# Scan states from split operands, and a new order around them, in an SSM block followed by an attention and recurrence block

## The chip, the cores and the metric

The kernel runs on one core of a Trainium2 chip. The metric is the device time of one execution in microseconds (us); the kernel before takes 2063.22 us (median of three runs, 2062.61 to 2064.13). Work is spread over engines that each run their own instructions in the order in which they are written: TensorE (PE: matmuls; PEld: its weight loads), VectorE (DVE), ScalarE (ACT), GpSimd (POOL) and SyncE (SP), which here issues nearly all DMAs.

## The reference

Two blocks over 512 positions of width 2048, in float32. What the change touches is the first block's mixer: a projection, a causal convolution with silu, and a scan over chunks that is computed with matmuls. For each group (8 of them, 8 heads each, one B and one C per group):

```
cs = cumsum(ac)                                     # per chunk
decay = exp(where(mask, cs[:, None] - cs[None, :], -inf))
y_diag = (C B^T) * decay @ xdt
y_off  = C @ state * exp(cs)
state  = state * exp(cs[-1]) + B^T @ (xdt * exp(cs[-1] - cs))
y = y_diag + y_off + d_skip * x;   y = y * silu(z)
```

The second block needs mod = silu(c) @ w_ada + b_ada, a vector of 6144 numbers, for shift, scale and gate. It does not depend on x, so the kernel computes it beside the first block.

## The kernel before, in words

Large products are exact to nearly float32 by splitting: each operand is written as hi (float32r, a ScalarE copy, L171) plus lo (the rest, a VectorE subtraction, L172), and three float32r matmuls make one product: hi*hi, hi*lo, lo*hi (L197 to L199, in `gemm`). Weights come in blocks of 512 KB (tile `raw`), and each block gives two pairs hi, lo; three buffers of each are in use, so that ScalarE's next hi copy waits until TensorE is through with the pair of three copies ago. A gemm of two output tiles (`g`) runs over 16 steps of the contraction, kt = 0 to 15, six matmuls each.

The first part works through 8 groups. Each group has five gemms: B and C; then for the first half of its heads x and z; then for the second half x and z. I call each half a unit, numbered 0 to 15: unit 2g is group g's first half, 2g+1 its second. The scan of unit u is put between the gemms:

- `bc_late`: transposes B (`btp`), copies it to `btok` (L517), and makes C B^T (`cbp`), masked into `cbm`. It stands at kt = 11 of the first x gemm of a group.
- `ssd_pre`: transposes x (`tp`), and makes xdt (x times dt) and xdw (x times the weight of the position at its chunk's end). `ssd_decay` makes the masked decays `dec` and the `cex` on ScalarE and VectorE. `ssd_states` multiplies btok with xdw for three chunks (float32 matmuls into `sa` and `sb`, L1149) and carries the state from chunk to chunk on VectorE: a multiplication by `exl` (L1157) and an addition (L1159) per chunk, into `st`. They stand at kt = 11, 12 and 14 of the unit's z gemm (in unit 0 at kt = 5, 6 and 9 of a later gemm).
- `ssd_unit`, after the z gemm: 56 small matmuls into `yp`, chunk 3 first: first those of dec and xdt (L1198), then those of cex and st (L1200). The first L1200 needs the last state, so the end of the chain of three states.

`ada(n)` takes n rows of w_ada (tile `adaw`, two buffers) and makes each a column of mod with one VectorE instruction of 1024 columns (L1226) behind the last lo. At its first and 49th row it loads c, and makes silu of it on ScalarE and VectorE (L1217 to L1221). There are two or three rows per gemm.

The program is recorded in this order, and a scheduler orders each engine's instructions by its own estimate of when each can start; `issue_after` and `high_priority` bind or favour some. PSUM pools: `pg` (the gemms), `pa` (tp, sa, sb, btp, cbp and others) and `py` (yp), two buffers each.

Of the kernel before, what the change touches and what calls it, by code (L numbers as in the profile page):

```python
# [6 lines left out]
F32 = mybir.dt.float32  # L7
F32R = mybir.dt.float32r
I32 = mybir.dt.int32
AF = mybir.ActivationFunctionType  # L10
# [130 lines left out]
class _K:  # L141
    def __init__(self, tc, I, O, dbg):
        self.tc, self.nc, self.I, self.O, self.dbg = tc, tc.nc, I, O, dbg
        self.n = 0

# [32 lines left out]
    def gemm(self, chunks, acts, ncol=2, nk=4, tag=0, before=None, early=True, after=None):  # L178
        nc = self.nc
        ps = [self.pg.tile([P, S], F32, tag=f"g{j + tag}", name=self.nm("g")) for j in range(ncol)]  # L180
        self.mms = []
        nkt = len(chunks) * nk
        kt = 0
        width = ncol * P
        for src in chunks:
            if before:
                before(kt)
            hl = self.wchunk(src, width * nk, early=early)
            for k in range(nk):
                if after:  # L190
                    after(kt)
                a = acts[kt]
                hi, lo = hl[k * 2 // nk]
                for j in range(ncol):
                    o = k % (nk // 2) * width + j * P
                    c = slice(o, o + P)
                    nc.tensor.matmul(ps[j], hi[:, c], a[:, 0, :], start=kt == 0, stop=False)  # L197
                    nc.tensor.matmul(ps[j], hi[:, c], a[:, 1, :], start=False, stop=False)  # L198
                    mm = nc.tensor.matmul(ps[j], lo[:, c], a[:, 0, :], start=False, stop=kt == nkt - 1)  # L199
                    self.mms.append(mm.ins)  # L200
                kt += 1
        assert kt == nkt
        return ps
# [160 lines left out]
    def part1(self):  # L364
# [138 lines left out]
        for g in range(NG):  # L503
# [6 lines left out]
            btok = tmp.tile([P, 3, P], F32, tag="btok", name=f"btok{g}", bufs=1)  # L510
            cbm = tmp.tile([P, NC, P], F32, tag="cbm", name=f"cbm{g}", bufs=1)

            def bc_late(g=g, bt=bt, ct=ct, btok=btok, cbm=cbm):
                btp = self.pa.tile([P, NC, P], F32, tag="a", name=f"btp{g}")
                for c in range(3):
                    nc.tensor.transpose(btp[:, c, :], bt[:, c * P : c * P + P], self.ckc("ident"))
                nc.scalar.activation(btok, btp[:, 0:3, :], AF.Copy)  # L517
                cbp = self.pa.tile([P, NC, P], F32, tag="a", name=f"cbp{g}")
                for c in range(NC):
                    nc.tensor.matmul(cbp[:, c, :], bt[:, c * P : c * P + P], ct[:, c * P : c * P + P],  # L520
                                     start=True, stop=True)
                nc.vector.tensor_tensor(cbm, cbp, self.ckc("triu").unsqueeze(1).to_broadcast([P, NC, P]), ALU.mult)
# [9 lines left out]
            for u in range(2):  # L532
# [21 lines left out]
                if g or u:  # L554
                    mid.update({11: steps[0:1], 12: steps[1:2], 14: steps[2:3]})
                    late.append(unit)
                else:
                    slow = {1: [bc_late], 5: steps[0:1], 6: steps[1:2], 9: steps[2:3]}
# [558 lines left out]
    def ssd_pre(self, g, u, xs, pre):  # L1117
# [5 lines left out]
        xdw = tmp.tile([P, 3, 4, 64], F32, tag="xdw", name=self.nm("xdw"), bufs=1)  # L1123
        for c2 in range(2):
            tp = self.pa.tile([P, 2, 4, 64], F32, tag="a", name=self.nm("tp"))
            for c in range(2):
                for j in range(2):
# [7 lines left out]
            nc.vector.tensor_tensor(xdw[:, a:b2], tp[:, 0 : b2 - a],  # L1135
                                    self.dtw[:, a:b2, h0 : h0 + 4].unsqueeze(3).to_broadcast([P, b2 - a, 4, 64]),
                                    ALU.mult)
        pre.update(csr=csr, xdt=xdt, xdw=xdw)


    def ssd_states(self, g, u, btok, pre):
# [6 lines left out]
        for c in range(3):  # L1148
            nc.tensor.matmul(parts[c].rearrange("p h d -> p (h d)"), btok[:, c, :],  # L1149
                             xdw[:, c].rearrange("p h d -> p (h d)"), start=True, stop=True)  # L1150
        st = []
        for c in range(3):
            ns = self.tmp.tile([P, 4, 64], F32, tag="st", name=self.nm("st"), bufs=3)
            if c == 0:
                nc.scalar.activation(ns, parts[0], AF.Copy)
            else:
                nc.vector.tensor_tensor(  # L1157
                    ns, st[-1], self.exl[:, c, h0 : h0 + 4].unsqueeze(2).to_broadcast([P, 4, 64]), ALU.mult)
                nc.vector.tensor_tensor(ns, ns, parts[c], ALU.add)  # L1159
# [26 lines left out]
    def ssd_unit(self, g, u, xs, pre, yg):  # L1186
# [4 lines left out]
        for c in (3, 2, 1, 0):  # L1191
            cl = slice(c * P, c * P + P)
            for part in range(2 if c else 1):
                for h in range(4):
# [6 lines left out]
                    prev = mm.ins  # L1201
        for j in range(2):
            nc.vector.scalar_tensor_tensor(yg[j], xs[j], self.pk("dskip", (g * 4 + u * 2 + j)), yp[j],
                                           ALU.mult, ALU.add)

    def ada(self, n):

        nc, I = self.nc, self.I
        for _ in range(n):
# [4 lines left out]
            kh, f = divmod(i, 48)  # L1214
            if f == 0:
                cb = self.tmp.tile([P, 1024], F32, tag="adac", name=self.nm("adac"), bufs=1)
                nc.sync.dma_start(cb, I["cvec"][kh].to_broadcast([P, 1024]))  # L1217
                th = self.tmp.tile([P, 1024], F32, tag="adaw", name=self.nm("adat"))
                nc.scalar.activation(th, cb, AF.Tanh, scale=0.5)
                nc.vector.scalar_tensor_tensor(cb, th, 1.0, cb, ALU.add, ALU.mult)  # L1220
                nc.vector.tensor_scalar(cb, cb, 0.5, None, ALU.mult)  # L1221
                self.cb = cb
            raw = self.tmp.tile([P, 1024], F32, tag="adaw", name=self.nm("adaw"))
            nc.sync.dma_start(raw, I["wada"][kh, f])
            with self.tc.issue_after(self.last_lo):
                nc.vector.tensor_tensor_reduce(out=raw, in0=raw, in1=self.cb, op0=ALU.mult, op1=ALU.add,  # L1226
                                               scale=1.0, scalar=0.0, accum_out=self.macc[:, i : i + 1])
            if i == 95:
# [23 lines left out]
```

## Time and profile before

| | |
|---|---|
| median of three runs | 2063.22 us |
| profiled execution | 2065.37 us |
| its span, first to last instruction | 2063.6 us |
| PE busy | 2042.9 us (99%) |
| DVE busy | 1316.8 us (64%) |
| ACT busy | 930.7 us (45%) |
| mean granted TensorE clock | 0.998 |

The groups and their scans take the span from about 62 us to 1001 us. "Busy" counts an instruction from its start to its modelled end; matmuls overlap, so the time that one costs is read from start to start in the timeline. Line numbers are those of the kernel before.

### The profile page before, as it was taken

The page shows a single profiled execution, that of the slowest core. Times are in us where ns is not written, and L with a number is a line of the kernel's source. Part 1 is how long each engine was busy: PE and PEld are TensorE (multiplying, and loading weights), DVE is VectorE, ACT ScalarE, POOL GpSimd, SP SyncE. Part 2 cuts the span into 40 slices and gives each one's busy share as a digit, 9 for nine tenths or more (in the row PEclk, how much of TensorE's full clock was granted, in tenths as well). Part 3 has the DMA queues.
Part 4 walks back from the last instruction along what each step waited for, and adds up shares of the span by engine and source line. Part 5 has one row for each costly group of instructions (what it writes and reads, how often), then busy time and mean ns, then how long its engine had stood idle before and what let it go on. Part 6 is the DMA issues. An engine that isn't in the chain of part 4 may idle for free.

```text
span 2063.6 us, 26879 instructions
## 1 busy us (share of the span) xinstructions
PE 2042.9 (99%) x10000; PEld 1694.2 (82%) x10000; DVE 1316.8 (64%) x2312; ACT 930.7 (45%) x1747; POOL 45.2 (2%) x35
## 2 busy tenths in 40 slices
PE   8999999999999999999999999989999999999999
PEld 7888888888878888888788888878888888888887
DVE  6777777687777868777643545476666675754333
ACT  6473444444344443444432433344554554763222
POOL 0000000000000000000000000000000000000000
PEclk9999999999999999999999999999999999999999
DMA  7344555545454454444533332225222223233442
GB/s 231 111 158 156 178 173 186 170 153 180 157 184 157 171 177 160 163 164 133 175 126 119 114 100 94 81 97 159 90 70 72 72 80 96 87 112 109 145 143 92
DMA packets 93268, 278.31 MB, mean 135 GB/s; under 512 B 9873, under 2 KB 20113, under 8 KB 91089
## 3 DMA queue, kind: packets, MB, share of 16 engines
q1 hardware_dynamic: 92848, 276.59, 41.0%
q8 instruction: 78, 1.28, 0.2%
q14 instruction: 54, 0.43, 0.1%
q10 hardware_dynamic: 288, 0.01, 0.0%
HBM read 262.80 MB, written 12.71 MB: 134 GB/s over the span
## 4 chain that ended last, share of the span: by engine, by line
PE 94%; DVE 3%; ACT 2%; DMA 1%; issue 1%; ACTq 0%; DVEq 0%
PE g L197 27%; PE g L198 27%; PE g L199 27%; PE yp L1198 1%; PE yp L1200 1%; PE gt L266 1%; PE gt L268 1%; PE gt L267 1%; PE op L926 1%; PE g L217 1%; DVE lo L172 1%; PE g L218 1%; PE g L219 1%; PE tp L1129 1%; PE sa L1149 1%
## 5 line engine op out<-in xcount | busy, mean ns | idle before, releaser
L172 DVE TENSOR_TENSOR lo<-raw,hi 128x512 fp32r<-128x512 f32 (+2 forms) x704 | 476.3, 677 | 542.3 <-ACT hi L171 539.6
L171 ACT ACTIVATE hi<-raw 128x512 fp32r<-128x512 f32 (+2 forms) x704 | 426.9, 607 | 860.9 <-PE g L198 774.6
L197 PE MATMUL g<-hn,hi 128*128 128x512 f32 x1216 | 480.0, 395 | 0.0
L199 PE MATMUL g<-hn,lo 128*128 128x512 f32 x1216 | 474.2, 390 | 0.0
L198 PE MATMUL g<-hn,hi 128*128 128x512 f32 x1216 | 473.9, 390 | 0.0
L197 PEld LDWEIGHTS g<-hn,hi 128*128 128x128 f32 x1216 | 228.3, 188 | 48.9 <-issue 2.4
L199 PEld LDWEIGHTS g<-hn,lo 128*128 128x128 f32 x1216 | 228.2, 188 | 48.0 <-issue 0.2
L198 PEld LDWEIGHTS g<-hn,hi 128*128 128x128 f32 x1216 | 228.4, 188 | 46.5 <-issue 0.2
L198 PE MATMUL g<-h,hi 128*128 128x512 f32 x512 | 200.7, 392 | 0.8 <-DVE h L689 0.8
L199 PE MATMUL g<-h,lo 128*128 128x512 f32 x512 | 199.8, 390 | 0.0
L197 PE MATMUL g<-h,hi 128*128 128x512 f32 x512 | 199.6, 393 | 0.0
L199 PE MATMUL g<-ya,lo 128*128 128x512 f32 x512 | 199.5, 390 | 0.0
L197 PE MATMUL g<-ya,hi 128*128 128x512 f32 x512 | 199.5, 390 | 0.0
L198 PE MATMUL g<-ya,hi 128*128 128x512 f32 x512 | 199.5, 390 | 0.0
L1226 DVE CUSTOM_DVE_ANT_0 adaw<-adaw,adac 128x1024 f32<-128x1024 f32 x96 | 115.6, 1221 | 18.7 <-DMA adaw<-in_wada 18.7
L198 PEld LDWEIGHTS g<-h,hi 128*128 128x128 f32 x512 | 96.2, 188 | 22.6 <-DVE h L689 3.2
L199 PEld LDWEIGHTS g<-ya,lo 128*128 128x128 f32 x512 | 96.1, 188 | 20.4 <-DVE lo L172 0.3
L197 PEld LDWEIGHTS g<-h,hi 128*128 128x128 f32 x512 | 96.0, 188 | 20.2 <-ACT h L688 1.1
L197 PEld LDWEIGHTS g<-ya,hi 128*128 128x128 f32 x512 | 96.1, 188 | 20.1 <-issue 0.2
L199 PEld LDWEIGHTS g<-h,lo 128*128 128x128 f32 x512 | 96.1, 188 | 19.9
L198 PEld LDWEIGHTS g<-ya,hi 128*128 128x128 f32 x512 | 96.1, 188 | 19.8 <-issue 0.2
L337 DVE SCALAR_TENSOR_TENSOR xc<-pr,cwh,xc 128x511 f32<-128x511 f32 (+1 forms) x144 | 101.8, 745 | 0.0
(362 smaller groups left out, 2597.2 us busy)
## 6 DMA issues: line engine op xcount, KB each, us to landing
raw<-in_win SPq DMA_DIRECT2D x216, 512.0 KB, 3.5
adaw<-in_wada SPq DMA_DIRECT2D x96, 512.0 KB, 4.6
raw<-in_wout SPq DMA_DIRECT2D x88, 512.0 KB, 3.5
csr<-csd SPq DMA_DIRECT2D x16, 1024.0 KB, 4.7
xT<-in_xT SPq DMA_DIRECT2D x16, 256.0 KB, 4.4
raw<-in_win SPq DMA_DIRECT2D x16, 256.0 KB, 3.6
ydram<-y SPq DMA_DIRECT2D x16, 256.0 KB, 2.1
yst<-ydram SPq DMA_DIRECT2D x8, 512.0 KB, 4.2
```

Source lines behind the costliest of these rows:

```text
L171: self.last_hi = nc.scalar.activation(hi, raw[:, i * h : i * h + h], AF.Copy).ins
L172: self.last_lo = nc.vector.tensor_tensor(lo, raw[:, i * h : i * h + h], hi.bitcast(F32), ALU.subtract).ins
L197: nc.tensor.matmul(ps[j], hi[:, c], a[:, 0, :], start=kt == 0, stop=False)
L198: nc.tensor.matmul(ps[j], hi[:, c], a[:, 1, :], start=False, stop=False)
L199: mm = nc.tensor.matmul(ps[j], lo[:, c], a[:, 0, :], start=False, stop=kt == nkt - 1)
L217: nc.tensor.matmul(ps[j], hi[:, o], a[:, 0, :], start=first, stop=False)
L218: nc.tensor.matmul(ps[j], hi[:, o], a[:, 1, :], start=False, stop=False)
L219: mm = nc.tensor.matmul(ps[j], lo[:, o], a[:, 0, :], start=False, stop=last)
L266: nc.tensor.matmul(ps[t], a[:, 0, ts], hi, start=k == 0, stop=False)
L267: nc.tensor.matmul(ps[t], a[:, 0, ts], lo, start=False, stop=False)
L337: nc.vector.scalar_tensor_tensor(xc[:, s:], ps[:, : S - s], w(k), xc[:, s:], ALU.mult, ALU.add)
L1226: nc.vector.tensor_tensor_reduce(out=raw, in0=raw, in1=self.cb, op0=ALU.mult, op1=ALU.add, scale=1.0, scalar=0.0, accum_out=self.macc[:, i ...
```

## The change

1. btok and xdw are split into hi and lo (float32r), and a product of the states is three float32r matmuls instead of one float32 matmul. New: a VectorE subtraction for btok; a float32 tile `xw` (one buffer), a ScalarE copy to hi and a VectorE subtraction to lo for each of the two pieces of xdw.
2. btp and cbp take buffers of `py` instead of `pa`.
3. The load of c for the second half of mod is issued at the 48th row, and that call of `ada` stops there; the silu of c is put behind the last lo.
4. In `ssd_states` the state instructions are recorded at high priority, and the first multiplication reads PSUM directly.
5. For second halves the three steps stand one kt earlier: 10, 11 and 13.
6. A fence: the first kt of the gemm after `ssd_unit` is issued behind the unit's last matmul.

```diff
@@ gemm
+                with self.tc.issue_after(self.fence) if self.fence is not None and kt == 0 else nullcontext():
...
+                self.fence = None
@@ part1
-            btok = tmp.tile([P, 3, P], F32, tag="btok", name=f"btok{g}", bufs=1)
+            btok = tmp.tile([P, 2, 3, P], F32R, tag="btok", name=f"btok{g}", bufs=1)
...
-                btp = self.pa.tile([P, NC, P], F32, tag="a", name=f"btp{g}")
+                btp = self.py.tile([P, NC, P], F32, tag="y", name=f"btp{g}")
...
-                nc.scalar.activation(btok, btp[:, 0:3, :], AF.Copy)
-                cbp = self.pa.tile([P, NC, P], F32, tag="a", name=f"cbp{g}")
+                nc.scalar.activation(btok[:, 0], btp[:, 0:3, :], AF.Copy)
+                nc.vector.tensor_tensor(btok[:, 1], btp[:, 0:3, :], btok[:, 0].bitcast(F32), ALU.subtract)
+                cbp = self.py.tile([P, NC, P], F32, tag="y", name=f"cbp{g}")
...
-                    mid.update({11: steps[0:1], 12: steps[1:2], 14: steps[2:3]})
+                    mid.update({10: steps[0:1], 11: steps[1:2], 13: steps[2:3]} if u else
+                               {11: steps[0:1], 12: steps[1:2], 14: steps[2:3]})
@@ ssd_pre
-            nc.vector.tensor_tensor(xdw[:, a:b2], tp[:, 0 : b2 - a],
+            xw = tmp.tile([P, 2, 4, 64], F32, tag="xw", name=self.nm("xw"), bufs=1)[:, 0 : b2 - a]
+            nc.vector.tensor_tensor(xw, tp[:, 0 : b2 - a],
...
+            nc.scalar.activation(xdw[:, 0, a:b2], xw, AF.Copy)
+            nc.vector.tensor_tensor(xdw[:, 1, a:b2], xw, xdw[:, 0, a:b2].bitcast(F32), ALU.subtract)
@@ ssd_states
-            nc.tensor.matmul(parts[c].rearrange("p h d -> p (h d)"), btok[:, c, :],
-                             xdw[:, c].rearrange("p h d -> p (h d)"), start=True, stop=True)
+            o = parts[c].rearrange("p h d -> p (h d)")
+            for i, (a, b) in enumerate(((0, 0), (0, 1), (1, 0))):
+                nc.tensor.matmul(o, btok[:, a, c, :], xdw[:, b, c].rearrange("p h d -> p (h d)"),
+                                 start=i == 0, stop=i == 2)
...
+            with self.tc.high_priority():
...
+                    nc.vector.tensor_tensor(ns, st[-1] if c > 1 else parts[0],
@@ ssd_unit
+        self.fence = prev
@@ ada
+            if i == 47:
+                self.ada_c(1)
+                return
```

Where instructions now stand, at three places. The first is VectorE in unit 2, from the last rows of mod in the z gemm to the last state. `adaw` are rows of mod, `lo` the gemm's lo tiles, the two `st` the second and third state, `zr` the first step on the z gemm's result. Before:

```order
L1226 ISA adaw_2052,macc<-adaw_2052,adac_1596 128x1024
L1226 ISA macc 128x1
L172 TENSOR_TENSOR lo_2064<-raw_2057,hi_2063 128x512
L1157 TENSOR_TENSOR st_1976<-st_1974,exl 128x256
L1159 TENSOR_TENSOR st_1976<-st_1976,sa_1969 128x256
L1157 TENSOR_TENSOR st_1979<-st_1976,exl 128x256
L1159 TENSOR_TENSOR st_1979<-st_1979,sb_1970 128x256
L567 TENSOR_TENSOR zr_2027<-g_1788,rb_602 128x512
```

The same place now (lines of the changed kernel: L173 is the lo, L1141 and L1145 the piece of xdw and its lo, L1168 and L1170 the states):

```order
L1244 ISA adaw_2087,macc<-adaw_2087,adac_1621 128x1024
L1244 ISA macc 128x1
L1141 TENSOR_TENSOR xw_1932<-tp_1926,dtw 128x256
L173 TENSOR_TENSOR lo_2102<-raw_2095,hi_2101 128x512
L1145 TENSOR_TENSOR xdw_1915<-xw_1932,xdw_1915 128x256
L1168 TENSOR_TENSOR st_2014<-sa_2001,exl 128x256
L1244 ISA adaw_2090,macc<-adaw_2090,adac_1621 128x1024
L1244 ISA macc 128x1
L1170 TENSOR_TENSOR st_2014<-st_2014,sa_2001 128x256
L572 TENSOR_TENSOR zr_2065<-g_1814,rb_602 128x512
L1168 TENSOR_TENSOR st_2017<-st_2014,exl 128x256
L173 TENSOR_TENSOR lo_2132<-raw_2129,hi_2131 128x512
```

The four state instructions stood together; now a row of mod stands behind the first, a step on z behind the second, the next gemm's lo behind the third, and the last addition (L1170 into st_2017) follows after that. Units 4, 6, 10, 12 and 14 show the same sequence.

The second place is TensorE at the start of unit 0's `yp`. Before, from the next gemm's first matmuls on:

```order
L199 MATMUL g_1179<-hn_104,lo_1183 128x512
L197 MATMUL g_1178<-hn_129,hi_1182 128x512
L198 MATMUL g_1178<-hn_129,hi_1182 128x512
L199 MATMUL g_1178<-hn_129,lo_1183 128x512
L1198 MATMUL yp_1136<-dec_1013,xdt_964 64x128 x2
L1198 MATMUL yp_1137<-dec_1013,xdt_964 64x128 x2
L1200 MATMUL yp_1136<-cex_1020,st_1061 64x128 x2
```

Now:

```order
L199 MATMUL g_900<-hn_543,hi_1101 128x512
L200 MATMUL g_900<-hn_543,hi_1101 128x512
L201 MATMUL g_900<-hn_543,lo_1102 128x512
L1209 MATMUL yp_1149<-dec_1020,xdt_965 64x128 x2
L1209 MATMUL yp_1150<-dec_1020,xdt_965 64x128 x2
L1211 MATMUL yp_1149<-cex_1027,st_1074 64x128 x2
```

Nine matmuls of the next gemm stood ahead of yp; now yp follows the last matmul of the gemm before it (g_900), and the nine come behind it. In unit 8 seven such matmuls, which stood between the first L1198 and the first L1200, have moved in the same way.

The third place is TensorE in unit 15, the last one, at its first L1200. Before, the last four of ten matmuls of the output projection stand ahead of it:

```order
L197 MATMUL g_8778<-ya_8785,hi_8798 128x512
L198 MATMUL g_8778<-ya_8785,hi_8798 128x512
L199 MATMUL g_8778<-ya_8785,lo_8799 128x512
L197 MATMUL g_8779<-ya_8785,hi_8798 128x512
L1200 MATMUL yp_8716<-cex_8676,st_8701 64x128 x2
L1200 MATMUL yp_8717<-cex_8676,st_8701 64x128 x2
```

Now:

```order
L201 MATMUL g_8693<-hn_543,lo_8864 128x512
L1209 MATMUL yp_8910<-dec_8841,xdt_8786 64x128 x2
L1209 MATMUL yp_8911<-dec_8841,xdt_8786 64x128 x2
L1159 MATMUL sb_8874<-xdw_8787,btok_8057 128x256 x3
L1211 MATMUL yp_8910<-cex_8848,st_8889 64x128 x2
L1211 MATMUL yp_8911<-cex_8848,st_8889 64x128 x2
```

All ten matmuls of the output projection (on `ya`) have left the gap between L1198 and L1200, and the three matmuls of the last chunk's state product, which stood a kt and more earlier, are in it.

## Rows read from the trace of the kernel before

**Rows 1.** Page, parts 1 and 2: busy time by engine; granted TensorE clock by slice.
```profile
PE 2042.9 (99%) x10000; PEld 1694.2 (82%) x10000; DVE 1316.8 (64%) x2312; ACT 930.7 (45%) x1747; POOL 45.2 (2%) x35
...
PEclk9999999999999999999999999999999999999999
```

**Rows 2.** Waits of TensorE: waiter, whom for, total us, times, longest us.
```profile
PE yp L1200 <- DVE st L1159: 3.8, 2, 2.2
```

**Rows 3.** Groups by line and shape, TensorE: count, busy us, mean ns.
```profile
L1149 PE MATMUL sa<-xdw,btok 128*128 128x256 f32 x64 | 16.5, 379 | 0.0
...
L1149 PE MATMUL sb<-xdw,btok 128*128 128x256 f32 x32 | 9.6, 381 | 0.0
```

**Rows 4.** Timeline, unit 2, TensorE: start us, duration us, instruction, count.
```profile
207.17 1.03 PE L1149 MATMUL sa<-xdw,btok 128*128 128x256 f32 x4
...
208.69 0.40 PE L198 MATMUL g<-hn,hi 128*128 128x512 f32 x1
...
211.32 0.66 PE L1198 MATMUL yp<-dec,xdt 128*64 128x128 f32 x8
211.81 0.62 PE L1200 MATMUL yp<-cex,st 128*64 128x128 f32 x8
```

**Rows 5.** Timeline, attention scores, TensorE: float32r matmuls of 256 columns.
```profile
1499.06 0.28 PE L886 MATMUL sp<-kh,qh 128*128 128x256 f32 x1
...
1499.54 0.40 PE L197 MATMUL g<-h,hi 128*128 128x512 f32 x1
```

**Rows 6.** Timeline, unit 2, VectorE.
```profile
203.20 0.69 DVE L1132 TENSOR_TENSOR xdt<-tp,dt 128x512 f32<-128x512 f32 x1
...
205.08 0.69 DVE L172 TENSOR_TENSOR lo<-raw,hi 128x512 fp32r<-128x512 f32 x1
205.68 0.42 DVE L1135 TENSOR_TENSOR xdw<-tp,dtw 128x256 f32<-128x256 f32 x1
206.02 1.22 DVE L1226 CUSTOM_DVE_ANT_0 adaw<-adaw,adac 128x1024 f32<-128x1024 f32 x1
...
208.03 1.23 DVE L1226 CUSTOM_DVE_ANT_0 adaw<-adaw,adac 128x1024 f32<-128x1024 f32 x1 [0.78 <-DMA adaw<-in_wada]
...
209.18 0.69 DVE L172 TENSOR_TENSOR lo<-raw,hi 128x512 fp32r<-128x512 f32 x1
...
211.29 0.42 DVE L1159 TENSOR_TENSOR st<-st,sb 128x256 f32<-128x256 f32 x1
```

**Rows 7.** Timeline, unit 2, ScalarE.
```profile
207.13 0.63 ACT L171 ACTIVATE hi<-raw 128x512 fp32r<-128x512 f32 x1 [2.09 <-PE g L198]
...
211.20 0.63 ACT L171 ACTIVATE hi<-raw 128x512 fp32r<-128x512 f32 x1 [2.58 <-DVE st L1157]
```

**Rows 8.** Timeline, unit 8, ScalarE and TensorE.
```profile
575.28 1.06 ACT L1219 ACTIVATE adat<-adac 128x1024 f32<-128x1024 f32 x1 [4.84 <-DMA adac<-in_cvec]
...
581.39 0.66 PE L1200 MATMUL yp<-cex,st 128*64 128x128 f32 x8 [2.19 <-DVE st L1159]
```

**Rows 9.** Timeline, unit 0, ScalarE and TensorE.
```profile
102.16 1.28 ACT L1173 ACTIVATE dec<-csr,cs 128x128 f32<-128x128 f32 x4 [0.16 <-DMA csr<-csd]
...
112.08 0.62 ACT L1175 ACTIVATE dec<-dec 128x512 f32<-128x512 f32 x1
...
111.41 0.39 PE L197 MATMUL g<-hn,hi 128*128 128x512 f32 x1
...
113.64 0.66 PE L1198 MATMUL yp<-dec,xdt 128*64 128x128 f32 x8
```

**Rows 10.** Timeline, unit 15, VectorE and TensorE.
```profile
993.09 0.75 DVE L599 SCALAR_TENSOR_TENSOR ya<-yst,pkt,ya 128x512 fp32r<-128x512 f32 x1 [0.34 <-ACT ya L598]
...
998.39 0.66 PE L1200 MATMUL yp<-cex,st 128*64 128x128 f32 x8 [1.59 <-DVE st L1159]
```

**Rows 11.** Windows: length us, busy us of PE, PEld, DVE, ACT, POOL, granted clock, DMA.
```profile
574.00:582.00 8.00, 5.81 (x40) 4.19 (x40) 5.63 (x11) 4.18 (x10) 0.00 (x0) 1.00 0.47 173
...
1356.00:1364.00 8.00, 5.80 (x25) 5.53 (x26) 3.91 (x18) 1.71 (x4) 0.00 (x0) 0.50 0.00 0
```

More of the change, by code (lines that the diff above doesn't have):

```diff
@@ L193, in gemm @@
                 hi, lo = hl[k * 2 // nk]
[L194 to L200, printed above, removed]
+                with self.tc.issue_after(self.fence) if self.fence is not None and kt == 0 else nullcontext():
+                    for j in range(ncol):
+                        o = k % (nk // 2) * width + j * P
+                        c = slice(o, o + P)
+                        nc.tensor.matmul(ps[j], hi[:, c], a[:, 0, :], start=kt == 0, stop=False)
+                        nc.tensor.matmul(ps[j], hi[:, c], a[:, 1, :], start=False, stop=False)
+                        mm = nc.tensor.matmul(ps[j], lo[:, c], a[:, 0, :], start=False, stop=kt == nkt - 1)
+                        self.mms.append(mm.ins)
+                self.fence = None
                 kt += 1
@@ L1122, in ssd_pre @@
         xdt = tmp.tile([P, NC, 4, 64], F32, tag="xdt", name=self.nm("xdt"), bufs=1)
-        xdw = tmp.tile([P, 3, 4, 64], F32, tag="xdw", name=self.nm("xdw"), bufs=1)
+        xdw = tmp.tile([P, 2, 3, 4, 64], F32R, tag="xdw", name=self.nm("xdw"), bufs=1)
         for c2 in range(2):
@@ L1153, in ssd_states @@
             ns = self.tmp.tile([P, 4, 64], F32, tag="st", name=self.nm("st"), bufs=3)
[L1154 to L1159, printed above, removed]
+            with self.tc.high_priority():
+                if c == 0:
+                    nc.scalar.activation(ns, parts[0], AF.Copy)
+                else:
+                    nc.vector.tensor_tensor(ns, st[-1] if c > 1 else parts[0],
+                                            self.exl[:, c, h0 : h0 + 4].unsqueeze(2).to_broadcast([P, 4, 64]), ALU.mult)
+                    nc.vector.tensor_tensor(ns, ns, parts[c], ALU.add)
             st.append(ns)
@@ L1204, in ssd_unit, with ada_c @@
                                            ALU.mult, ALU.add)
+    def ada_c(self, kh):
+        self.cb = self.tmp.tile([P, 1024], F32, tag="adac", name=self.nm("adac"), bufs=1)
+        self.nc.sync.dma_start(self.cb, self.I["cvec"][kh].to_broadcast([P, 1024]))
     def ada(self, n):
@@ L1214, in ada @@
             kh, f = divmod(i, 48)
+            if i == 0:
+                self.ada_c(0)
             if f == 0:
[L1216 to L1222, printed above, removed]
+                cb = self.cb
+                with self.tc.issue_after(self.last_lo):
+                    th = self.tmp.tile([P, 1024], F32, tag="adaw", name=self.nm("adat"))
+                    nc.scalar.activation(th, cb, AF.Tanh, scale=0.5)
+                    nc.vector.scalar_tensor_tensor(cb, th, 1.0, cb, ALU.add, ALU.mult)
+                    nc.vector.tensor_scalar(cb, cb, 0.5, None, ALU.mult)
             raw = self.tmp.tile([P, 1024], F32, tag="adaw", name=self.nm("adaw"))
```

## The prediction

> **What bounds the kernel now.** I read the page first: the share of busy time by engine and the clock. TensorE is busy 99% of the span and at full clock (2.4 GHz) throughout [rows 1]. So a change is worth what it takes from TensorE's matmuls or waits, and costs what it adds to them; VectorE and ScalarE count only where TensorE comes to wait for them. Next the waits of TensorE. In all the scans it waits for a state twice, 3.8 us together [rows 2]. The timeline shows where: in unit 8 for 2.19 us, behind the silu of c, which ScalarE began 4.84 us late because c was still being loaded [rows 8]; and in unit 15 for 1.59 us [rows 10]. Everywhere else the states are ready in time, though barely: in unit 2 the last addition starts at 211.29, takes 0.42, and the matmul that needs it starts at 211.81 [rows 4, 6]. That is the place to watch: any further delay of the last state is a delay of TensorE. All times below are absolute times of the profiled execution; I lay the changed order over them.
>
> **State products.** Each unit has six float32 passes (96 in all, two per product) [rows 3]. From 207.17 to 208.69, less one gemm matmul of 0.23, the block costs 1.29 us [rows 4]; the 0.23 is the mean of the eleven matmuls from 208.69 to 211.32 with the step to yp. Nine float32r matmuls of 256 columns replace them. The scores have four of these from 1499.06 to 1499.54, 0.12 each [rows 5]; nine take 1.08. So a unit gains 0.21 us, 16 units 3.4 us. Bounds: nothing, if nine weight loads in a row are dearer than there, and 0.4 a unit if the switch of formats after the block falls away as well.
>
> The Trainium skill says in FP8 and Floating Point Precision (TensorE Precision Notes) that true float32 takes four passes through the array. By that, three products are 3/4 of 1.29 and a unit would gain 0.32 us, or 5.2 in all, an estimate from that page; the rows give a little less, since a pass of 256 columns has some fixed cost, and the sum goes by the rows.
>
> **Even units from 2 to 14 without unit 8 (six of them).** VectorE's order there is the first place shown in the section on the change. Durations, start to next start: 512 columns 0.60 (205.08 to 205.68), 256 columns 0.34 (205.68 to 206.02), a row of mod 1.15 (208.03 to 209.18), the last addition 0.42 to its end [rows 6]. From 203.20: xdt, xw, xdt to 205.00; lo at 205.08, when its hi is there; the lo of xdw to 206.28; a row of mod to 207.43; the second xw to 207.77; lo (its hi copy runs from 207.13 for 0.63 [rows 7]) to 208.41; the second lo of xdw to 208.75, just in time for sb; a state multiplication to 209.09; a row of mod, whose load is there since 208.03, to 210.24; addition to 210.58; step on z to 211.18; multiplication to 211.52; then the lo of the next gemm. Its hi waits for TensorE's last matmuls on the buffer, 211.20 before [rows 7] and 0.21 earlier now, and is done at 211.62: lo to 212.26. Only then the last addition, done at 212.68. TensorE could start at 211.81 - 0.21 = 211.60 and starts at about 212.75: a wait of 1.15 us. Net against before: 212.75 - 211.81 = +0.94, for six units **+5.6 us**. What hid the state before was that its four instructions stood ahead of z and lo. Bounds: +0.3 a unit (VectorE gets ahead by one 512-column step) to +1.6 (the row of mod waits for its load again, 0.78 as at 208.03).
>
> **Odd units from 3 to 13 (six).** Transposes come one kt (1.36 us) earlier, and the row of mod, lo and lo of xdw stand ahead of the last addition as well, but no step on z and no further lo. With the same durations, from the end of the transposes: lo 0.50, xdt, xw, xdt 2.30, row of mod 3.45, lo 4.07, lo of xdw 4.67, row of mod 5.82, xw 6.15, two state steps 6.98, lo 7.58, state step 7.91, lo of xdw 8.24, row of mod 9.4 to 9.5, addition 9.90. TensorE gets there at 9.84, so it waits about 0.1 us. Net -0.1 each, **-0.6 us**; bounds -0.2 and +0.8 each (its row of mod is read as soon as it lands).
>
> **Unit 0.** Before, nine gemm matmuls from 111.41 on covered the time until the decays were ready at 113.64 [rows 9]. Now yp stands ahead of them, so TensorE is there at 111.2. ScalarE makes the decays without a pause from 102.16 to 112.70 [rows 9]; the hi copy that stood within this stretch now stands at its head, and waits for TensorE until about 103.0. The same work then ends at 113.5, VectorE's last decay after two steps of 0.6 at about 114.4, and TensorE waits 3.2 us. Against before: 0.8 later, and nine matmuls of 0.23 still to do: **+2.85 us**. Bounds: +2.0 (the hi copy costs nothing) to +4.
>
> **Unit 8.** No row of mod and no silu of c stand between its state steps; by the even units' sum its last addition is done a microsecond before TensorE needs it, even without the seven matmuls that covered it. The 2.19 us go, and 0.21: **-2.4 us**. **Unit 1**: -0.2.
>
> **Unit 15.** VectorE now runs between ya tiles that wait for their loads: from the one at 993.09 [rows 10], 0.3 us earlier, ya 0.66, addition 0.34, ya 0.66, multiplication 0.34, ya 0.66, lo 0.60, the second xw 0.34, a step on z 0.60, its lo 0.34 to 997.4. Then TensorE's last two products of sb, and the last addition, to about 998.4. The first L1200 thus starts at 998.4 as before [rows 10], but the ten matmuls that covered the time are still to do: **+2.3 us**. Bounds: 0 and +4.
>
> **Hidden edits.** The copies of xdw and the lo of btok (0.5 us per group) lie in ScalarE's and VectorE's idle time away from the states. The earlier load of c is counted in unit 8, the moved silu of c in the first x gemms costs nothing while lo tiles are two buffers ahead. The PSUM pools change no order that TensorE waits on.
>
> **Sum.** 5.6 - 0.6 + 2.85 - 2.4 - 0.2 + 2.3 = +7.5 us. The profiled execution took 2065.37 (span 2063.6 and 1.8 around it), so 2072.9 by its clock; the median of the runs is 2.15 lower, and the prediction is 2063.2 + 7.5 = **2070.7 us**. About 0.2% (4.1 us) is what a measurement of this kernel tells from no change.
>
> **Rivals.** (a) The states are in time everywhere. For it: they are recorded at high priority, and VectorE is idle a third of the time [rows 1]. Against: the order has a row of mod, z and lo between them. It decides at 211.55 in unit 2: if the last addition ends by then, 1.1 us earlier than I sum. Then 3.4 + 2.2 + 1.6 = 7.2 go: 2056.0. Chance 0.13. (b) Only the lost covers cost: even units do not wait, units 0 and 15 do. 2.85 + 2.3 - 2.4 - 0.2 - 12 x 0.21 = 0: 2063.2. Chance 0.20. (c) Slower still: the long wait in unit 0 brings the clock down. After waits of TensorE for the sums between the blocks the granted clock was 0.50 (1.2 GHz) for 8 us, while after the 2.19 us of unit 8 it stayed at 1.00 [rows 11]. The wait in unit 0 is longer than the latter. At half clock the 2.9 us of yp would take twice as long: 2070.7 + 3 = 2073.7. Chance 0.10. TensorE: Matmul & The Clock Gate in the Trainium skill (Part 1: The HAM clock gate) says that idleness takes the clock to half and sustained work gives it back; both rows agree with that. That the change does not do what it says is part of the forecast: the state updates do not come first.
>
> **How the numbers follow.** Forecast 0.57, own range 2067.5 to 2073. Slower by over 0.2% (above 2067.3): the forecast but for 0.04 of it, and (c): 0.63. Within: (b) and 0.06 of the rest: 0.24. Faster: 0.13. The range that holds 8 in 10 leaves out (a) and a little above: 2060 to 2075.
>
> **What would show it.** TensorE's waits for the last state addition (now L1170) about 1.1 us in each of units 2, 4, 6, 10, 12, 14, near 0 in the odd ones and in unit 8; 3 us in unit 0, on the last decay; 4 us in unit 15, part of it at sa and sb; state products at 0.12 each; no idle time before the silu of c on VectorE. No waits in the even units would make the prediction wrong.

## The result and the profile after

The changed kernel took 2077.2 us, the median of four runs (2074.27 to 2078.26), beside 2063.68 us for the kernel before; the ratio is 1.0059, 95% interval 1.0047 to 1.0071. It is slower, as forecast, but by 13.5 us instead of 7.5, and above the range of 2060 to 2075. Five runs taken later gave 2075.0 against 2063.86, ratio 1.0053 [1.0040, 1.0067].

The profiled execution is the shortest of the four: 2074.27 us, span 2072.5, that is 8.9 more than before. The nine runs order themselves by the mean granted clock of TensorE: two at 0.998 (mean 2074.0 us), three at 0.997 (2075.1), three at 0.996 (2077.3), one at 0.995 (2078.3). The kernel before has 0.998 in nearly every run. So the trace accounts for 8.9 us, and the clock is the first place to look for what the other runs have more. It is not the whole of the spread: the runs of the kernel before that stood beside those five have 0.998 and lie between 2061.28 and 2065.74 us.

The page of the kernel after, parts 1 and 2, beside [rows 1]: TensorE is busy 0.6 us less, in a span 8.9 us longer. It does less work and waits more. The slices are too coarse to show the clock.

```profile
PE 2042.3 (99%) x10048; PEld 1691.0 (82%) x10048; DVE 1333.5 (64%) x2352; ACT 944.8 (46%) x1779; POOL 50.9 (2%) x35
...
PEclk9999999999999999999999999999999999999999
```

Its waits of TensorE (waiter, whom for, total us, times, longest), beside [rows 2], where the states cost 3.8 us in two places:

```profile
PE yp L1211 <- DVE st L1170: 7.5, 8, 1.0
...
PE yp L1209 <- DVE dec L1187: 3.4, 1, 3.4
...
PE sb L1159 <- ACT xdw L1144: 1.5, 1, 1.5
```

Eight waits for the last state addition are the six even units, unit 8 and unit 15. The wait for the decay is unit 0's. Timeline of unit 2, VectorE, beside [rows 6] (start us, duration us, instruction, count):

```profile
211.74 0.42 DVE L1141 TENSOR_TENSOR xw<-tp,dtw 128x256 f32<-128x256 f32 x1
212.17 0.69 DVE L173 TENSOR_TENSOR lo<-raw,hi 128x512 fp32r<-128x512 f32 x1
212.78 0.42 DVE L1145 TENSOR_TENSOR xdw<-xw,xdw 128x256 fp32r<-128x256 f32 x1
213.11 0.41 DVE L1168 TENSOR_TENSOR st<-sa,exl 128x256 f32<-128x256 f32 x1
213.45 1.21 DVE L1244 CUSTOM_DVE_ANT_0 adaw<-adaw,adac 128x1024 f32<-128x1024 f32 x1
...
214.59 0.41 DVE L1170 TENSOR_TENSOR st<-st,sa 128x256 f32<-128x256 f32 x1
214.96 0.69 DVE L572 TENSOR_TENSOR zr<-g,rb 128x512 f32<-128x512 f32 x1
215.56 0.41 DVE L1168 TENSOR_TENSOR st<-st,exl 128x256 f32<-128x256 f32 x1
216.12 0.69 DVE L173 TENSOR_TENSOR lo<-raw,hi 128x512 fp32r<-128x512 f32 x1
216.74 0.41 DVE L1170 TENSOR_TENSOR st<-st,sb 128x256 f32<-128x256 f32 x1
```

This is the order laid out in the forecast: a row of the modulation, z and lo between four state instructions. The last addition starts 1.2 us after the first yp (215.53). Unit 0, TensorE, beside [rows 9]:

```profile
111.07 0.39 PE L201 MATMUL g<-hn,lo 128*128 128x512 f32 x1
114.82 1.12 PE L1209 MATMUL yp<-dec,xdt 128*64 128x128 f32 x8 [3.36 <-DVE dec L1187]
115.72 1.07 PE L1211 MATMUL yp<-cex,st 128*64 128x128 f32 x8
...
118.41 0.60 PE L1211 MATMUL yp<-cex,st 128*64 128x128 f32 x8
118.85 0.60 PE L1209 MATMUL yp<-dec,xdt 128*64 128x128 f32 x8
```

From one row of eight to the next it takes 0.90 us at first and 0.44 at the end: the clock was down. Windows (length, busy us of PE, PEld, DVE, ACT, POOL, granted clock, DMA share, GB/s), beside [rows 11]:

```profile
111.00:114.50 3.50, 0.46 (x3) 0.04 (x1) 3.50 (x7) 3.50 (x9) 0.00 (x0) 0.96 0.73 185
114.50:117.50 3.00, 2.68 (x26) 2.69 (x28) 3.00 (x6) 0.60 (x1) 0.00 (x0) 0.50 0.76 309
```

Unit 8, ScalarE, beside [rows 8]:

```profile
579.82 0.63 ACT L172 ACTIVATE hi<-raw 128x512 fp32r<-128x512 f32 x1
581.94 1.06 ACT L1238 ACTIVATE adat<-adac 128x1024 f32<-128x1024 f32 x1 [1.49 <-DMA adac<-in_cvec]
582.90 0.37 ACT L1166 ACTIVATE st<-sa 128x256 f32<-128x256 f32 x1
```

ScalarE still waits for c there, and the copy of the first state stands behind it; TensorE then waits 0.87 us for the state. Unit 15, TensorE, beside [rows 10]:

```profile
1002.74 0.66 PE L1209 MATMUL yp<-dec,xdt 128*64 128x128 f32 x8
1004.91 0.98 PE L1159 MATMUL sb<-xdw,btok 128*128 128x256 f32 x3 [1.51 <-ACT xdw L1144]
1006.41 0.66 PE L1211 MATMUL yp<-cex,st 128*64 128x128 f32 x8 [0.51 <-DVE st L1170]
```

**Step by step.** The gemm matmuls stand in the same order in both kernels, so the start of each can be subtracted from the start of the same one before; the growth of that shift from one unit to the next is what a unit costs.

| stretch | forecast | first trace |
|---|---|---|
| start, up to unit 0 | 0 | -0.1 |
| units 0 and 1 | +2.85 - 0.2 | +4.4, of it about 1.4 the clock |
| 2, 4, 6, 10, 12, 14 | +5.6 | +6.2 (0.89 to 1.15 each) |
| 3, 5, 7, 9, 11, 13 | -0.6 | +0.2 |
| 8 | -2.4 | -1.8 |
| 15 | +2.3 | +1.2 |
| sums between the blocks | 0 | -1.4 |
| rest | 0 | +0.2 |
| sum | +7.5 | +8.9 |

The 1.4 are worked out from the rows above: some 14 steps of yp, two matmuls each, at 0.21 us (0.85 for four) instead of 0.11 (0.44 for four). Experiment 1 gives the same in another way. The sums got cheaper by luck: behind their waits the clock was at 1.2 GHz for 10.2 us before and for 6.8 us after, and both values turn up again in other traces in which nothing was changed there (10.2 in 6 and 11, 6.8 in 10).

### The profile page after: what moved, and what is told of

Same layout as the page of the kernel before. It is cut to its first block, busy times and chain, and to the rows that moved or that the text cites. A ratio compares the mean times of both kernels' runs of the same rounds, so it can differ in the third digit from the quotient of the medians.

```text
span 2072.5 us, 27025 instructions
## 1 busy us (share of the span) xinstructions
PE 2042.3 (99%) x10048; PEld 1691.0 (82%) x10048; DVE 1333.5 (64%) x2352; ACT 944.8 (46%) x1779; POOL 50.9 (2%) x35
## 4 chain that ended last, share of the span: by engine, by line
PE 93%; DVE 3%; ACT 2%; issue 1%; DMA 1%; SPq 0%; DVEq 0%; ACTq 0%
PE g L199 27%; PE g L200 26%; PE g L201 26%; PE yp L1209 1%; PE yp L1211 1%; PE gt L269 1%; PE gt L271 1%; PE gt L270 1%; PE op L931 1%; DVE lo L173 1%; PE tp L1134 1%; PE g L222 1%; PE g L220 1%; PE g L221 1%; PE sa L1159 1%
## 5 line engine op out<-in xcount | busy, mean ns | idle before, releaser
L173 DVE TENSOR_TENSOR lo<-raw,hi 128x512 fp32r<-128x512 f32 (+2 forms) x704 | 478.1, 679 | 538.3 <-ACT hi L172 533.0
L340 DVE SCALAR_TENSOR_TENSOR xc<-pr,cwh,xc 128x511 f32<-128x511 f32 (+2 forms) x144 | 101.9, 743 | 0.2
```

The lines of the kernel that those rows point to most:

```text
L173: self.last_lo = nc.vector.tensor_tensor(lo, raw[:, i * h : i * h + h], hi.bitcast(F32), ALU.subtract).ins
L340: nc.vector.scalar_tensor_tensor(xc[:, s:], ps[:, : S - s], w(k), xc[:, s:], ALU.mult, ALU.add)
```

## Experiments

Shifts are against the first trace of the kernel before, in us, and come from the profiled execution; medians are of 4 to 11 runs, ratios against runs of the kernel before on the same chip. Waits and steps are as in the table above.

### Is it the clock, and where?

**1. The changed kernel again**, no edit.

> The changed kernel once more, unaltered, as the yardstick for the three beside it and for a second look at its clock. Theory C (the granted clock falls in unit 0 behind TensorE's 3.4 us wait, and in most runs longer than in the profiled one): median about 2077, mean granted clock 0.995 to 0.996 in most runs against 0.998 for the kernel before, and where the profiled run has that lower clock, its extra time at 1.2 GHz lies in unit 0 (from about 114 on). Theory S: the extra lies at the sums between the blocks (about 1360 to 1374) instead, and unit 0 shows 3 us of it as in the first profile.

2075.0 us. In its profiled execution (clock 0.998) TensorE waits for the decay in unit 0 for 3.36 us as in the first, and the clock does not fall; it falls in unit 15 instead, where it had held:

```profile
114.50:117.50 3.00, 2.45 (x45) 2.46 (x46) 3.00 (x5) 0.82 (x2) 0.00 (x0) 1.00 0.86 322
...
1004.00:1007.00 3.00, 2.49 (x22) 2.19 (x23) 2.79 (x6) 2.26 (x5) 0.00 (x0) 0.51 0.91 345
```

Units 0 and 1 cost +3.1 here, 1.3 less than in the first trace, and unit 15 +2.6, 1.4 more: a fall is worth about 1.4 us. Neither theory had this: the same wait of the same program brings a fall in one execution and none in the other, and there is a second place, unit 15. The Trainium skill (TensorE: Matmul & The Clock Gate, Part 1: The HAM clock gate) says that the monitor behind the gate runs freely and does not start with the kernel. That one wait of 3.36 us had two outcomes fits this, but does not show it.

**2. Matmuls not held behind yp in unit 0.**

```
-        self.fence = prev
+        self.fence = prev if g or u else None
```

> The order that holds the next block's first matmuls behind yp is dropped for unit 0 alone; units 1 to 15 keep it. In unit 0 nine matmuls stand ahead of yp again, as in the kernel before. Theory C: the 3.4 us wait shrinks to under 1.5 us, the clock stays at 2.4 GHz through yp, the first profile's step of unit 0 (+4.6 us) goes, and the mean granted clock is 0.998 again in all runs: 2069 to 2072. Theory S: only the wait's 2.4 us go, the runs stay at a mean clock of 0.995 to 0.996: 2074.5.

2070.1 us, 1.0029 [1.0018, 1.0041]; five of six runs at 0.998. Units 0 and 1 cost -0.1. As theory C has it.

**3. Unit 0's wait filled.** 14 matmuls into the tile that yp then overwrites, ahead of yp.

```
+        if g == 0 and u == 0:
+            prev = self.mms[-1]
+            for _ in range(14):
+                with tc.issue_after(prev):
+                    mm = nc.tensor.matmul(yp[0], self.hn0[:, 0, 0:P], self.hn0[:, 1, :], start=True, stop=True)
+                prev = mm.ins
```

> Unit 0's wait stays, but 14 matmuls of 512 columns (0.22 us each, about 3.1 us; their result is overwritten) run in it just ahead of yp. Nothing of the kernel's own work moves. Theory C: the clock stays at 2.4 GHz, yp's steps stay at 0.11 us, mean clock 0.998, and the time falls by 2.1 us at least (what the first profile lost to the clock) and up to 5: 2072 to 2075. Rival W (the wait itself is the whole cost and the clock matters little): no change, 2077.

2073.42 us, 1.0044 [1.0031, 1.0057], runs within 1.4 us of each other. The wait's length is there, yp runs at full clock (a row 0.44 after the last):

```profile
110.68 3.33 PE L1207 MATMUL yp<-hn 128*128 128x512 f32 x14
114.18 0.66 PE L1216 MATMUL yp<-dec,xdt 128*64 128x128 f32 x8 [0.16 <-DVE dec L1188]
114.66 0.61 PE L1218 MATMUL yp<-cex,st 128*64 128x128 f32 x8
```

Against the 2075.0 of the unfilled kernel that is 1.6 us, about one fall, though the two intervals overlap. The traces are clearer: units 0 and 1 cost +3.0 with the wait filled, +3.1 unfilled without a fall (1) and +4.4 with one. So a fall costs something in unit 0, but the wait, worth 3.1 us by experiment 2, costs more.

**4. Nothing but the held matmuls**, added to the kernel before (the same `fence` lines in gemm and ssd_unit).

> The kernel before, with nothing but the order that holds the next block's first matmuls behind yp. Theory F (each of the three places with covering matmuls loses them: 2.0 us in unit 0, 1.6 in unit 8, 2.3 in unit 15, and the longer waits let the clock fall in some runs, 1.5 to 2 us each): 2070 to 2073, some runs at a mean clock under 0.998. Rival G (the matmuls only change places with yp and TensorE has other work that fills the wait): 2064 to 2066.

2074.23 us, 1.0044 [1.0032, 1.0057]; clocks 0.995 to 0.997. In the trace unit 0 waits 2.15 us, unit 8 3.46 and unit 15 3.93, and the clock falls behind all three. Theory F, and 1.2 us above its range. This part of the change alone costs 10.4 us, nearly as much as the whole change.

How long the clock was at 1.2 GHz in each trace, in us, added up from windows of half a microsecond, with the waits that stand ahead of it:

| kernel | unit 0: wait, low clock | unit 15: low clock | sums |
|---|---|---|---|
| before | covered, 0 | 0 | 10.2 |
| after | 3.36, 3.4 | 0 | 6.8 |
| after again (1) | 3.36, 0 | 3.4 | 6.8 |
| not held in unit 0 (2) | covered, 0 | 3.4 | 6.8 |
| unit 0 filled (3) | filled, 0 | 3.4 | 6.8 |
| held, before (4) | 2.15, 3.4 (and 3.4 in unit 8) | 3.4 | 10.2 |
| states ahead (6) | 3.4, 6.8 | 0 (no long wait there) | 10.2 |
| steps one kt later (8) | 3.4, 0 | 3.4 | 6.8 |
| silu behind the copy (11) | 3.3, 6.8 | 3.4 | 10.2 |

In unit 15 two waits stand ahead of a fall, one of 1.4 to 2.5 us for xdw and, three matmuls later, one of 0.5 (in 4 a single one of 3.9). No trace has a fall behind the 1.0 us waits of the even units, nor behind the 2.19 and 2.01 us of unit 8 in the kernel before and in 10; in 4, unit 8 waits 3.46 us and has one.

### What covers the waits

**5. No matmuls held in any unit** of the changed kernel (the line that sets `fence` left out).

> The order that holds the next block's first matmuls behind yp is dropped in all units; then nine matmuls stand ahead of yp in unit 0, six (1.36 us) behind its first four in units 2, 4, 6, 10, 12 and 14, 16 in unit 15. Theory C with my sum: 4.5 to 7 us from unit 0, and the six even units' waits of 1.0 us are covered, 6.2 us: 2064 to 2067. Rival: the covering matmuls only move the wait to the lo tiles that come later on VectorE, and the even units gain nothing: 2070 to 2073.

2067.86 us, 1.0018 [1.0009, 1.0027]. The even units cost +0.05 to +0.25 now, the odd ones +0.3 to +0.5: one gemm matmul stands in yp there, and each change of shape costs TensorE about 0.1 (the rows of experiment 9 show one). The cover works nearly as summed (0.9 us above the range of theory C), and the kernel is still slower than before.

### What makes the states late

**6. The states really ahead.** Rows of the modulation of a z block and the step on z behind the last state addition; matmuls still held.

```
+                    mid[15] = [lambda: self.ada(3, self.last_st)]
...
+                    with tc.issue_after(self.last_st) if g else nullcontext():
+                        nc.vector.tensor_tensor(zr, ps[j], self.rb0, ALU.mult)
```

> The changed kernel, with the state updates really ahead on VectorE: the rows of the modulation of a z block and the first step on z are held behind the last state addition. All else stays, the order that holds matmuls behind yp too. Theory O (the six even units wait 1.0 us each because a row of the modulation, z and lo stand between the state updates; unit 8 waits 0.9 us because a silu of c stands ahead of its state copy on ScalarE): these seven waits go, 6.2 + 0.9 us, the waits in units 0 and 15 stay: 2067.5 to 2069. Rival L (the updates are late because of the split itself, xw, its copy and its lo ahead of them): the waits stay at 0.7 us or more: 2073.

2064.52 us, 1.0001 [0.9992, 1.0010], although its trace has 6.8 us of low clock in unit 0. All waits for states but 0.2 us are gone; units 2 to 14 cost -7.3 where they cost +4.6. Theory O, and more: the difference of 11.9 is 4.8 above the 7.1 of the waits, and the time is 3 us under the range. The nine products of a unit also stand together again; how much of the 4.8 that is was not separated.

**7. The same with no matmuls held.**

> As the kernel with the states ahead, and the next block's first matmuls no longer held behind yp (nine cover unit 0 again, five unit 15, none the others). Theory O: no waits for states are left but in unit 15, the gain of the float32r products (0.21 us a unit, 3.4 in all) and of unit 8 (2.2 us) shows: 2057.5 to 2060, faster than both kernels. Rival L: 2063 or more.

2056.95 us (2056.59 to 2057.39), 0.9964 [0.9951, 0.9978]: faster than both kernels, half a microsecond under the range of theory O, all runs at 0.998. Units 2 to 7 and 9 to 14 cost -0.25 to -0.51 each. Unit 2, VectorE and TensorE:

```profile
208.22 0.42 DVE L1169 TENSOR_TENSOR st<-sa,exl 128x256 f32<-128x256 f32 x1
208.68 0.42 DVE L1171 TENSOR_TENSOR st<-st,sa 128x256 f32<-128x256 f32 x1
209.13 0.42 DVE L1169 TENSOR_TENSOR st<-st,exl 128x256 f32<-128x256 f32 x1
209.66 0.42 DVE L1171 TENSOR_TENSOR st<-st,sb 128x256 f32<-128x256 f32 x1
```

```profile
206.89 0.87 PE L1160 MATMUL sa<-xdw,btok 128*128 128x256 f32 x6
207.60 0.52 PE L1160 MATMUL sb<-xdw,btok 128*128 128x256 f32 x3
207.96 0.39 PE L199 MATMUL g<-hn,hi 128*128 128x512 f32 x1
```

The four state instructions follow each other, and the last ends at 210.08, before yp starts (210.78). Nine products take 207.96 - 206.89 = 1.07 us; the forecast had 1.08.

**8. The second unit's steps one kt later**, as in the kernel before.

```
-                    mid.update({10: steps[0:1], 11: steps[1:2], 13: steps[2:3]} if u else
-                               {11: steps[0:1], 12: steps[1:2], 14: steps[2:3]})
+                    mid.update({11: steps[0:1], 12: steps[1:2], 14: steps[2:3]})
```

> The changed kernel with the steps of a group's second unit one kt later, where the kernel before has them. Theory O: it was the earlier step that kept the odd units in time; now units 3, 5, 7, 9, 11 and 13 have VectorE's order of the even ones and wait 1.0 us each: 2075 + 6 = 2081. Rival: the odd units have time to spare, 2075 to 2076.

2081.14 us, 1.0086 [1.0072, 1.0100]. Theory O: the odd units cost +0.93 to +1.17 each, and the waits read:

```profile
PE yp L1210 <- DVE st L1169: 14.0, 14, 1.3
```

**9. Nothing but the split products**, in the kernel before.

> The kernel before, with nothing but the state products as three float32r products of split operands (nine of 256 columns a unit in place of six float32 passes) and what makes the operands. VectorE's order of the state updates becomes that of the changed kernel's even units in units 2 to 7 and 9 to 14, and five gemm matmuls (1.13 us) stand behind the first four of yp there, as the kernel before allows. Theory O: without those five, each of the twelve units would wait 1.0 us, as the changed kernel's even units do; the five cover it, and 0.21 to 0.36 us a unit are gained: 2058 to 2061. Rival: the states are later than the cover lasts, or the two changes of matmul format cost as much as the products save: 2063 to 2066.

2065.85 us, 1.0011 [1.0002, 1.0020]. The rival: units 2 to 7 and 9 to 14 cost +0.04 to +0.30. The cover holds, but costs as much as the products save:

```profile
212.24 0.66 PE L1204 MATMUL yp<-dec,xdt 128*64 128x128 f32 x8
212.83 0.50 PE L197 MATMUL g<-hn,hi 128*128 128x512 f32 x1
213.17 0.40 PE L198 MATMUL g<-hn,hi 128*128 128x512 f32 x1
...
214.20 0.66 PE L1206 MATMUL yp<-cex,st 128*64 128x128 f32 x8
```

Without cover the second row of yp stands 0.49 behind the first [rows 4]; here it is 1.96, five matmuls of 0.23 and 0.33 more. The nine products also stand in three pieces here.

### Unit 8

**10. Nothing but row c a block ahead**, in the kernel before (ada and ada_c as after).

> The kernel before, with row c of the modulation loaded a block ahead and its silu behind a lo tile, nothing else. The seven matmuls that covered unit 8 stand behind yp here. Theory: the 2.2 us wait of unit 8 goes: 2061.5. Rival: the load is no earlier than the buffer comes free, the silu of c on ScalarE stands ahead of the state copy of unit 8, and 0.9 us or more of wait stays: 2062.6 to 2064.

2065.35 us, 1.0002 [0.9993, 1.0011]. The rival (the median is above its range too, the traced run of 2062.78 within). The load leaves at 567.9 (568.7 before, and the whole trace is 0.8 ahead there), so it is no earlier: its buffer comes free with the last row that uses it. The silu still stands ahead of the state copy, and unit 8 waits 2.01 us in place of 2.19:

```profile
574.02 1.06 ACT L1225 ACTIVATE adat<-adac 128x1024 f32<-128x1024 f32 x1 [4.39 <-DMA adac<-in_cvec]
574.99 0.61 ACT L171 ACTIVATE hi<-raw 128x512 fp32r<-128x512 f32 x1
575.51 0.36 ACT L1155 ACTIVATE st<-sa 128x256 f32<-128x256 f32 x1
```

**11. The silu behind the state copy** in the changed kernel.

```
+                with self.tc.issue_after(self.last_cp if kh else self.last_lo):
                     th = self.tmp.tile([P, 1024], F32, tag="adaw", name=self.nm("adat"))
                     nc.scalar.activation(th, cb, AF.Tanh, scale=0.5)
+                with self.tc.issue_after(self.last_st if kh else self.last_lo):
```

> The changed kernel with the silu of the modulation's second c held behind the state copy on ScalarE (and behind the last state addition on VectorE) in unit 8; nothing else moves. Theory T (ScalarE waits 1.5 us for that load and only then copies the state): unit 8's wait of 0.9 us goes, the time falls to about 2074. Rival: the wait stays, because VectorE's additions or the lo tile there are late by themselves: 2075.

Unit 8 costs -2.87 where it cost -1.83, and waits for nothing, although ScalarE still waits 1.05 us for c: theory T, in the trace. What the silu ahead of the copy costs differs from one execution to the next with how late c lands. In the second trace of the unaltered changed kernel (1) ScalarE waits 0.87 us and TensorE only 0.26:

```profile
580.19 1.06 ACT L1238 ACTIVATE adat<-adac 128x1024 f32<-128x1024 f32 x1 [0.87 <-DMA adac<-in_cvec]
583.47 0.66 PE L1211 MATMUL yp<-cex,st 128*64 128x128 f32 x8 [0.26 <-DVE st L1170]
```

Unit 8 cost -2.44 there, -2.66 and -2.75 in 2 and 3, where it does not wait, and -1.65 in 8, where it waits 1.05. The median, 2077.13 us, shows none of it: these runs had clocks of 0.995 to 0.997, the traced one low stretches of 20.5 us in all. One microsecond is not to be read from medians of this kernel.

### Waits and clock apart

**12. The kernel of 7 with products of the constants in the two waits for the sums**, five and four.

> The kernel with the states ahead and no held matmuls, and besides float32 products of the constants (their result is read by nobody) in TensorE's two waits for the sums between the blocks: five of 512 columns in the first, four in the second. Theory C (what a fall of the clock costs is half of 3.4 us each time, and the sums bring two of them in this kernel): the clock stays at 2.4 GHz there, 2 to 3.4 us go: 2053.5 to 2055. Rival: the waits were the whole cost, 2057; or the added products delay the sums, 2058.

2059.05 us, clock 1.00, 2 us slower than without them (in the traces the stretch of the sums is 1.6 us longer). The size was wrong: a float32 product of 512 columns, two rows of the trace, takes 0.86 us, so five end at 1349.23, where the sums could start at 1347.66 in 7:

```profile
1344.94 4.45 PE L675 MATMUL fill<-ckt 128*128 128x512 f32 x10
1349.23 1.84 PE L298 MATMUL sx<-ckt,q 128*128 128x1 f32 x16
```

**13. The same with three and two.**

> The kernel with the states ahead and no held matmuls, with three and two products of the constants in the two waits for the sums; five and four ran beyond the waits and made the kernel slower. Theory C: 2054 to 2055.5, mean clock 1.00. Rival (that stretch is bounded by the additions of the sums and h): 2056.5 to 2057.5, no gain over the kernel without them.

2056.62 us (2056.46 to 2059.32), 0.9969 [0.9958, 0.9980], clock 1.00: nothing gained over 7 that the medians can tell. In the traces the stretch of the sums is 0.9 us shorter than in 7, where it had 6.8 us of low clock.

**14. Three and two in the kernel before.**

> The kernel before with the products of the constants in the two waits for the sums, three and two of 0.86 us, sized to end before each wait does. Theory C: the clock stays at 2.4 GHz there, two or three falls of 3.4 us go, 2060 to 2062. Rival: the falls cost nothing because the additions of the sums and h bound that stretch, 2063.5.

2062.22 us, 0.9991 [0.9982, 1.0000], clock 1.00: 1.8 us less than the 2064.06 beside it. In the traces the stretch of the sums is 2.4 us shorter than before, where it had 10.2 us of low clock.

**15. The changed kernel with all four places filled.**

> The changed kernel with matmuls whose result is overwritten or read by nobody in all four places where the traces so far showed the clock fall: 14 of 0.22 us in unit 0's wait, two of some 0.65 us in unit 15's, three and two of 0.86 us in the waits for the sums. The kernel's own work stays in order. Theory C (beyond the waits, which the first profile sums to 7.8 us net, the rest of what the change costs is the clock): mean clock 1.00 in every run, runs within 1.5 us of each other, and the distance to the kernel before with the same products at the sums is 7 to 8.5 us: 2067 to 2070. Rival (something else adds to the runs that were longer than the profiled one): the distance stays 11 us or more.

2071.83 us, 1.0039 [1.0026, 1.0052], clock 1.00 in four runs and 0.999 in one, runs within 2.0 us. The distance to 14 is 9.6 us, between the two expectations. With the clock up in both, this is what the change costs without falls, mainly waits. In the two traces it is 10.9: 0.5 ahead of unit 0, 3.4 in units 0 and 1, 5.0 in units 2 to 14, 1.7 in unit 15, 0.2 behind. Of the 11.2 and 13.5 us that the medians differ by, then, about 9.6 are there without the clock and 1.6 to 3.9 are the clock; runs of one kernel that spread over 2 to 4 us give no finer split.

## Why the prediction was wrong

TensorE's two waits for the sums between the blocks, in the kernel before (waiter, whom for, total us, times, longest):

```profile
PE sx L295 <- ACT q L648: 2.6, 1, 2.6
PE rr L304 <- DVE r L285: 2.2, 1, 2.2
```

- **The step that failed** is rival (c), the fall of the clock: the sum has it at nothing, its chance was 0.10, and it was looked for in unit 0 only. The forecast set the 2.19 us of unit 8 at full clock [rows 11] against it. But the two waits between the blocks, behind which it read a clock of 0.50, were 2.6 and 2.2 us long, hardly longer, and the 3.2 us forecast for unit 0 were longer than both. The price of (c), 3 us, is that of two stretches of 3.4 us (5.98 for units 0 and 1 in 6, where 3.06 is the cost without a fall); one costs 1.4. The traces show low stretches in unit 0, behind waits of 2.15 to 3.4 us, in four of six executions, in unit 15 in six of the seven with matmuls held that wait there, and the sums vary by 3.4 us. The range to 2075 left no room for falls in several places, and that the runs of the changed kernel would spread over 4 us was not seen.
- **How much that is.** The first median is 6.0 us above the forecast's +7.5. By 15, 3.9 of them are the clock, and 2.1 are terms that were too small (9.6 instead of 7.5), above all in units 2 to 14 (5.0 in the traces of 15, 4.6 in the first, 2.6 forecast). Without the clock the changed kernel would be at 2063.7 + 9.6 = 2073.3 us, an estimate from these medians, and inside the range.
- **Full clock throughout** [rows 1] was a misreading: a digit 9 means 90% or more, and the kernel before has 10.2 us at 1.2 GHz at the sums, as [rows 11] shows in part.
- **Subtracting 2.15 us** from profile to median took for granted that the profiled execution after the change would lie as far above its median as the one before. It lay 2.9 us under it, being one of those with the least low clock.
- **Unit 8**: -2.4 forecast, -1.8 and -2.4 measured in the two traces of the changed kernel. The statement that the earlier load is counted there failed. The load is not earlier (10), and its silu still stands ahead of the state copy on ScalarE (11); whether TensorE waits for that depends on when c lands. What unit 8 did gain seems to come from the order, in which hi, lo and the silu's steps no longer stand ahead of or between the state instructions; this is read from the two orders, and no run separates it.
- **Odd units**: -0.6 forecast, +0.2 measured. The position of the steps kept them in time, as forecast (8). But the nine products stand in four pieces between gemm matmuls there (three in the even units), each change costs about 0.1 us, and the gain of 0.21 is gone. Where the nine stand together, as in 7, a unit gains 0.25 to 0.51, more than the 0.21 of the forecast.
- **Unit 15**: +2.3 forecast without a fall. Without one it is +1.2, with one +2.5 to +3.1; that the forecast lies between is luck.
- **Right**: the even units (+0.94 forecast, 0.89 to 1.15 measured) and why they wait (6, 7); unit 0's wait (3.2 and 3.36); the price of nine products (1.08 and 1.07); that the state updates do not come first.
- **Rivals**: (a) is out for the changed kernel. Its 2056.0 left out that unit 0 waits for a decay and not for a state: with the states ahead and the matmuls still held the time is 2064.5 (6), and only without holding them 2057.0 (7). (b) is out, since the even units wait. In the chances the rest that lies within 0.2% is once 0.04 and once 0.06; the sum goes by 0.04.

## What to carry to other kernels

Asking for an instruction early by priority doesn't put it ahead: read the order, and order it behind or ahead by name, as the kernel of 7 does; with that, and with no matmuls held, the rest of the change gains 7 us where the whole lost 11 and more. Don't forbid a matmul to move ahead of a wait, unless nothing waits there. Where TensorE can come to wait some 2 us or more (in unit 15, 1.4 and 0.5 us close together were enough), expect the clock to fall in some executions and not in others: read the mean granted clock of every run before explaining medians by a trace, and give the range one fall for each such wait.

## What was not expected of the hardware

One program with one and the same wait of 3.36 us ran on at 2.4 GHz in one execution and at 1.2 GHz in the other. One low stretch of 3.4 us costs about 1.4 us, as the runs show too: from a mean clock of 0.998 to one of 0.995 they are 4.3 us longer, and two traces of the changed kernel at 0.998 have 10.2 us of low clock where those at 0.995 (of 4 and 11) have 20.5, three stretches more. Filling the two waits for the sums is worth 1.8 us in the kernel before and nothing measurable in the kernel of 7. In part this is because the latter had less low clock there to lose (6.8 us instead of 10.2, and 0.9 us gained in the trace instead of 2.4); the rest stays open. A float32 product of 512 columns takes 0.86 us and a float32r matmul of as many 0.23, a ratio of 3.8; the Trainium skill's four passes for true float32 (FP8 and Floating Point Precision, TensorE Precision Notes) fit that, and the forecast's price by rows, 1.08, fits the 1.07.
